# A mixture of 32 experts in 16 pairs: four places for a pair's rows, weights in 8 KB packets, another order at the end

## The chip, the cores and the metric

The kernel runs on one core of one Trainium2 chip. The metric is the device time of one execution in microseconds (us); lower is better. Engines are named as in the profile: PE multiplies matrices, PEld is its loading of weights, DVE and ACT work on vectors, POOL works on vectors and issues indirect DMAs, SP issues the other DMAs.

## The reference

One block for 512 tokens of width 1024, in float32: a state-space mixer and a latent attention side by side, a cross attention into 256 memory rows, a hierarchical mixture of experts, and a final norm. The change touches the last two:

```
x = x + _hier_moe(_rms(x, norm_moe_g), ...)
    # a token chooses 1 of 4 groups of experts, then 2 of the 8 experts in it; for each:
    # out += gate_weight * (silu(t @ w_gate[e]) * (t @ w_up[e])) @ w_down[e]
return _rms(x, norm_final_g)
```

An expert has w_gate and w_up of 1024 x 256 and w_down of 256 x 1024, 3 MB together, so 32 experts are 96 MB of weights. The final norm divides a row by the root of the mean of its squares and multiplies it by a gain.

## The kernel before

**Pairs.** The experts are worked in 16 pairs. Each expert has 64 places for tokens (`CAP`), so a pair has 128, one per partition. Which token has which place is found by the router; an index table `IX` says for each pair which rows of `hd` (the tokens in memory) to gather, `IY` where its results go. A token's first result goes to `xd` (which starts as x itself), the second to `yd`.

**Stages of a pair n.** `get` (L1768) transposes the gathered rows on PE (tile pX) and DVE copies them out with the gain (XT). `first` (L1780) multiplies by gate and up of both experts into pG (128 places by 512: 256 gate columns, 256 up columns); ACT takes SiLU of the gate half (sl, L1806), DVE multiplies by the up half (a, L1812). `second` transposes that (pA, L1830), ACT copies it out (aT, L1832), and PE multiplies by down (pD, L1846). DVE adds the rows that were already scaled (YY, L1855), except for pairs 14 and 15, whose sums are made on PE at the end. The main loop runs `first(n)`, then `second(n - 1)`, so that products of two pairs alternate on PE.

**Rows on POOL.** There are two places for gathered tokens, XG[0] and XG[1], and one tile YY with two halves for results (`result`, L1816). In `first(n)` POOL scales the tokens of pair n into their half of YY (L1808), then gathers the tokens of pair n + 2 into the place just read (L1699). `second(n - 1)` ends with two scatters of the half of YY to xd and yd (L1861). POOL does these in program order: scale, gather, scatter, scatter.

**Weights on SP.** `load_to` (L1303) issues the loads of weights on SP in a fixed turn, ahead of their use, into buffers that come free as PE is done with them. A tile `gu` holds half of the depth of both matrices: index c = 0 has k = 0 to 3 of each group of eight rows of gate and of up, c = 1 has k = 4 to 7. It takes two DMAs of 512 KB (L1310 gate, L1311 up) whose runs are 4 KB per partition. The down weights of an expert are one DMA of 1 MB (L1323) in runs of 8 KB, the last two of them in halves. One product step takes 64 places of one expert against 512 columns, gate and up at once (L1789), which the profile shows as two PE instructions.

**The end.** When the scatter of pair 13 has landed, `take_back` (L1872) reads yd and xd back, eight DMAs of 512 KB, and `both(t)` adds the two for each of four groups of 128 tokens, t = 0 to 3, on DVE (L1944). `last_sum` puts the results of pairs 14 and 15 onto the tokens with PE (pC; L1920, and for t = 2 and 3 also the tokens themselves by an identity, L1914). Then the order `TO` runs: a (L1929) adds pC to the tokens for t = 0, 1 in two halves; s takes squares and their sums on ACT (L329) half by half; o scales on DVE (L1940) and issues the output. Last, DVE copies the four pC tiles of t = 2, 3 into the tokens (L1961), for an expert that ran out of places; the branch for it is not taken in the profiled execution.

Of the kernel before, what the change touches and what calls it, by code (L numbers as in the profile page):

```python
# [15 lines left out]
AF = mybir.ActivationFunctionType  # L16
# [3 lines left out]
S = 512  # L20
# [42 lines left out]
OBJ = 3  # L63
OQ = '00-01-10-P2-11-20-C0-C1-C2-P3-C3-21-30-31'.split('-')
TQ = 1
TO = 'a00 s00 a01 s01 a10 s10 a11 s11 o00 o01 s20 s21 o10 o11 s30 s31 o20 o21 o30 o31'.split()
FH = 1
T1 = 1
CM = 1
# [4 lines left out]
PL0 = {(3,0):0,(3,2):1}  # L74
CP = 3
CB = 1
G1 = 6
FE = 0
LS = 0
LC = 2  # L80
# [24 lines left out]
def build(tc, I, out, dbg=None, stop=None):  # L105
# [1185 lines left out]
    def slot(tag, shape, name, dt=F32):  # L1291
        if tag == "A":
            return ua(shape, dt, name)
        if tag in "EG":
            return (E[0] if tag == "E" else GP_).tile(shape, dt, name=name, tag=tag)
        if tag in "FY":
            return MP.tile(shape, dt, name=name, tag=tag, bufs=NF if tag == "F" else 1)
        return u("H" if tag == "X" else tag, shape, dt, name)
# [3 lines left out]
    def load_to(n):  # L1302
        while nld[0] < min(n, 96):  # L1303
            i = turn[nld[0]]
            nld[0] += 1
            e, c = order[i]
            tag = tags[i]
            if c < 2:
                t = slot(tag, [128, 2, 4, 256], f"gu{e}{c}")
                nc.sync.dma_start(t[:, 0], wgt[e, :, 4 * c:4 * c + 4])  # L1310
                nc.sync.dma_start(t[:, 1], wup[e, :, 4 * c:4 * c + 4])  # L1311
            else:
                t = slot(tag, [128, 2, D], f"dn{e}")
                if i == 94:
                    late.append((t, e))
                    nc.sync.dma_start(t[:, :, 0:512], wdn[e][:, :, 0:512])
                elif i == 95:
                    late.append((t, e))
                    nc.sync.dma_start(t[:, :, 0:512], wdn[e][:, :, 0:512])
                    for t_, e_ in late:  # L1320
                        nc.sync.dma_start(t_[:, :, 512:D], wdn[e_][:, :, 512:D])
                else:
                    nc.sync.dma_start(t, wdn[e])  # L1323
            ew[e, c] = t
# [368 lines left out]
    if at("router"):  # L1693
        return

    stage = {}

    def gather(n):
        gat.append(nc.gpsimd.indirect_dma_start(out=XG[n % 2], out_offset=None, in_=hd,  # L1699
                                                in_offset=bass.IndirectOffsetOnAxis(ap=IX[:, n:n + 1], axis=0),  # L1700
                                                bounds_check=S - 1, oob_is_err=False))

# [53 lines left out]

    silu, YY, lastd = [None], [], {}
    turns = {}  # L1760

    def turn_(k, i):
# [3 lines left out]
    xts_ = {0: dict(enumerate(xt0))}  # L1766

    def get(n, c):  # L1768
        xg = XG[n % 2].rearrange("t (p k) -> t k p", k=8)
        ps = bankt(f"pX{n}{c}")  # L1770
        for k in range(4):
            i = nc.tensor.transpose(ps[:, k * 128:k * 128 + 128], xg[:, 4 * c + k], ident)  # L1772
            behind(i, last[0])
            behind(i, lastd.get(n - 2))
        if n == 1:
            last[0] = i
        xt = half_T(n, c)
        xts_.setdefault(n, {})[c] = xt
        evac_T(xt, ps, c)

    def first(n, mid=None):
        xt = xts_.setdefault(n, {})
        pg = bank2(f"pG{n}", "a") if n else bank("pG0")

        def mul(k0, k1):
            for k in range(k0, k1):
                c, kk = divmod(k, 4)
                for s in range(2):
                    i = nc.tensor.matmul(pg[64 * s:64 * s + 64], xt[c][:, kk, 64 * s:64 * s + 64],  # L1789
                                         ew[2 * n + s, c][:, :, kk], start=k == 0, stop=k == 7)  # L1790
                    behind(i, last[0])
            last[0] = i

        if n == 0:
            mul(0, G1)
            get(1, 0)
            mul(G1, 8)
        else:
            if n > 1:
                get(n, 0)  # L1800
            get(n, 1)
            if mid is not None:
                next(mid)
            mul(0, 8)
        sl = MP.tile([128, 256], F32, name=f"sl{n}", tag="sl", bufs=1)
        silu[0] = nc.scalar.activation(sl, pg[:, 0:256], AF.Silu, scale=RS[:, n:n + 1])  # L1806
        if 0 < n < NS:
            nc.gpsimd.tensor_scalar(result(n), XG[n % 2], F1[:, n:n + 1], 1.0, OP.mult, OP.mult)  # L1808
        if n and n + 2 < 16:
            gather(n + 2)  # L1810
        a = MP.tile([128, 2, 128], F32, name=f"a{n}", tag="a", bufs=1)
        stt.append(v.scalar_tensor_tensor(a.rearrange("s t p -> s p t"), pg[:, 256:512].rearrange("s (p t) -> s p t", t=2),  # L1812
                               RS[:, n:n + 1], sl.rearrange("s (p t) -> s p t", t=2), OP.mult, OP.mult))
        stage[n] = a

    def result(n):  # L1816
        if not YY:
            YY.append(slot("Y", [128, 2, D], "YY"))
        return YY[0][:, n % 2]

    def in_turn(n, i):
        if n > 13:
# [3 lines left out]
    def second(n):  # L1826
# [7 lines left out]
        if sums:  # L1834
            Y = slot(next(free), [128, 2, D], f"Y{n}", F32R)
            oht = MP.tile([128, S], F32R, name=f"oht{n}", tag="oht")
            v.tensor_scalar(oht, tokh, TK[:, n:n + 1], None, OP.is_equal)
            stage["y", n] = Y, oht
        else:
            Y = result(n)  # L1840
        yield at_i
        for c in range(2):
            pd = bank(f"pD{n}{c}")
# [81 lines left out]
    def fin_(k, t, c):  # L1925
        x = pc[t, c] if t in on_pe else X[t][:, half[c]]
        r = fst[:, 3, t:t + 1]
        if k == "a":
            turn_("v", v.tensor_tensor(x, x, pc[t, c], OP.add))  # L1929
        elif k == "s":  # L1930
            turn_("a", square_sum(fst[:, c, t:t + 1], x, spare[:, c]))
            if c == 0:
                turn_("a", nc.scalar.activation(fst[:, 2, t:t + 1], fst[:, 0, t:t + 1], AF.Copy, scale=1.0 / D, bias=EPS))
            else:
                turn_("a", nc.scalar.activation(r, fst[:, 1, t:t + 1], AF.Sqrt, scale=1.0 / D, bias=fst[:, 2, t:t + 1]))
        else:
            if c == 0:
                turn_("v", v.reciprocal(r, r))
            xg = (xg0, xg1)[c]
            turn_("v", v.scalar_tensor_tensor(xg[:, t], x, r, gf[:, half[c]], OP.mult, OP.mult))  # L1940
            nc.sync.dma_start(out[0, t * 128:t * 128 + 128, half[c]], xg[:, t])
# [5 lines left out]
    on_pe = (2, 3)  # L1947
    for i in down15:
        turn_("v", i)
    for t in range(NT):  # L1950
        both(t)
    for n, ts in ((14, (0, 1, 2, 3)), (15, (0, 1)), (None, (2,)), (15, (2,)), (None, (3,)), (15, (3,))):
        for t in ts:
            for c in range(2):
                last_sum(t, c, n)
    for q in TO:
        fin_(q[0], int(q[1]), int(q[2]))

    for t in on_pe:
        for c in range(2):  # L1960
            turn_("v", v.tensor_copy(X[t][:, half[c]], pc[t, c]))  # L1961
    overflow(*ov)
    es.close()

# [18 lines left out]
```

## Time and profile before

| what | value |
|---|---|
| time, median of 3 runs | 717.35 us (716.89 to 717.83) |
| the profiled execution: time | 717.67 us |
| its span | 715.9 us |
| its granted PE clock, mean | 0.984 |
| PE / DVE / ACT / POOL busy, share of the span | 93% / 57% / 35% / 16% |
| bytes by the hardware queue / the software queue | 157.58 MB / 7.58 MB |

The span is the time from the first to the last instruction of the profile; 1.8 us of the profiled execution lie outside it. The last of pair 15's products ends at about 686 us of the span. In the table by stretches the granted clock is a share of full speed. A wait in brackets is the idle time of the engine before the row, with the instruction whose end released it.

### The profile page before, as it was taken

Reading aid. Unit: us, or ns where it says so; the run is one execution under the profiler, and the core shown is the slowest. Engines: PE = TensorE matmul, PEld = TensorE weight load, DVE = VectorE, ACT = ScalarE, POOL = GpSimd, SP = SyncE. Lnnn points to the kernel's source line nnn. Section 1 sums busy time; section 2 is a strip of 40 time slices with the busy share of each in tenths; the row PEclk is TensorE's granted clock in tenths of the full one; section 3 lists DMA queues with packets and bytes.
Section 4 is the critical chain, followed back from the end, with each engine's and each line's share of the span. In section 5 each row is a group of like instructions: output and inputs, shape, how many; then the busy total and the mean of one; then the engine's idle time right before and its main releaser. Section 6 shows DMA issues by size and latency. Waiting matters only on the chain.

```text
span 715.9 us, 10163 instructions
## 1 busy us (share of the span) xinstructions
PE 666.9 (93%) x3644; PEld 469.7 (66%) x3644; DVE 406.1 (57%) x952; ACT 251.8 (35%) x518; POOL 113.7 (16%) x165
## 2 busy tenths in 40 slices
PE   5989999788999999999999999989999999999793
PEld 4788878676778888888887788734344454454342
DVE  4899988747577887565366642653443512221137
ACT  5734364325666767244344522221000000000023
POOL 6300022002400000102000001212242233233100
PEclk9999999989999999999999999999999999999988
DMA  7763233335452434323328797799999999999993
GB/s 217 199 197 99 66 79 95 79 124 125 112 191 67 147 120 118 95 83 89 91 87 314 274 334 276 240 395 410 405 412 406 411 412 404 410 411 409 381 356 128
DMA packets 102012, 165.83 MB, mean 232 GB/s; under 512 B 32762, under 2 KB 64606, under 8 KB 98120
## 3 DMA queue, kind: packets, MB, share of 16 engines
q1 hardware_dynamic: 95512, 157.58, 62.0%
q0 software_dynamic: 6432, 7.58, 3.1%
q8 instruction: 30, 0.49, 0.3%
q14 instruction: 22, 0.18, 0.1%
q10 hardware_dynamic: 16, 0.00, 0.0%
HBM read 154.59 MB, written 25.69 MB: 252 GB/s over the span
## 4 chain that ended last, share of the span: by engine, by line
PE 59%; DMA 28%; DVE 5%; ACT 4%; issue 1%; SPq 1%; POOL 1%; ACTq 0%; DVEq 0%
DMA gu<-moe_w_up 18%; DMA dn<-moe_w_down 6%; PE pG L1789 3%; PE po L1039 2%; PE pxq L268 2%; PE pxq L267 2%; PE pxq L266 2%; PE pxo L266 2%; DMA raw<-w_in 2%; PE pxo L267 2%; PE pD L1846 1%; PE pxo L268 1%; PE pcq L266 1%; PE pPT L1028 1%; PE pcq L267 1%
## 5 line engine op out<-in xcount | busy, mean ns | idle before, releaser
L1789 PE MATMUL pG<-gu,XT 128*64 128x512 f32 x512 | 120.3, 607 | 6.6 <-DMA gu<-moe_w_up 3.0
L214 DVE TENSOR_TENSOR lo<-raw,hi 128x1024 fp32r<-128x1024 f32 (+3 forms) x64 | 75.5, 1183 | 62.0 <-ACT hi L204 61.5
L204 ACT ACTIVATE hi<-raw 128x1024 fp32r<-128x1024 f32 (+3 forms) x64 | 63.9, 1002 | 107.9 <-issue 26.0
L1789 PEld LDWEIGHTS pG<-gu,XT 128*64 128x64 f32 x512 | 54.5, 139 | 58.7 <-issue 52.0
L1812 DVE SCALAR_TENSOR_TENSOR a<-pG,RS,sl 128x256 f32<-128x256 f32 x16 | 10.7, 671 | 113.2 <-ACT sl L1806 106.8
L1846 PE MATMUL pD<-dn,aT 128*64 128x512 f32 x256 | 71.1, 600 | 0.5 <-ACT aT L1832 0.5
L1806 ACT ACTIVATE sl<-pG,RS 128x256 f32<-128x256 f32 x16 | 7.6, 473 | 123.5 <-PE pG L1789 123.5
L1846 PEld LDWEIGHTS pD<-dn,aT 128*64 128x64 f32 x256 | 22.4, 137 | 35.7 <-issue 34.4
L1855 DVE SCALAR_TENSOR_TENSOR YY<-pD,GT,YY 128x512 f32<-128x512 f32 x26 | 19.5, 750 | 25.2 <-PE pD L1846 25.1
L1808 POOL TENSOR_SCALAR YY<-XG,F 128x1024 f32<-128x1024 f32 x13 | 14.5, 1116 | 114.8 <-issue 50.7
L1832 ACT ACTIVATE aT<-pA 128x256 f32<-128x256 f32 x16 | 6.1, 384 | 68.0 <-PE pA L1830 36.4
L1772 PEld LDWEIGHTS pX<-ident,XG 128*128 128x128 f32 x120 | 14.6, 194 | 16.9 <-issue 12.9
L267 PE MATMUL pxq<-gT,hi 128*128 128x512 f32 x64 | 25.6, 400 | 0.0
L266 PE MATMUL pxq<-gT,hi 128*128 128x512 f32 x64 | 25.5, 399 | 0.0
L268 PE MATMUL pxq<-gT,lo 128*128 128x512 f32 x64 | 25.4, 396 | 0.0
L1417 DVE TENSOR_TENSOR XT<-pX,gmo 128x512 f32<-128x512 f32 x30 | 19.3, 683 | 7.4 <-PE pX L1772 7.4
L1772 PE MATMUL pX<-ident,XG 128*128 128x128 f32 x120 | 17.6, 288 | 3.8 <-DMA XG<-hd,IX 3.8
L1388 POOL TENSOR_TENSOR st_moe<-st_moe 128x1 f32<-128x1 f32 x4 | 0.8, 190 | 118.6 <-issue 104.4
L266 PE MATMUL pcq<-hT,hi 128*128 128x512 f32 x48 | 19.2, 401 | 0.0
L268 PE MATMUL pcq<-hT,lo 128*128 128x512 f32 x48 | 19.1, 398 | 0.0
L267 PE MATMUL pxv<-lo,mT 128*128 128x512 f32 x32 | 13.9, 435 | 5.5 <-DVE lo L214 5.5
L267 PE MATMUL pcq<-hT,hi 128*128 128x512 f32 x48 | 18.9, 395 | 0.0
(614 smaller groups left out, 1670.6 us busy)
## 6 DMA issues: line engine op xcount, KB each, us to landing
gu<-moe_w_gate SPq DMA_DIRECT2D x64, 512.0 KB
gu<-moe_w_up SPq DMA_DIRECT2D x64, 512.0 KB
dn<-moe_w_down SPq DMA_DIRECT2D x30, 1024.0 KB
raw<-w_in SPq DMA_DIRECT2D x9, 512.0 KB
raw<-xattn_w_v SPq DMA_DIRECT2D x8, 512.0 KB
raw<-xattn_w_k SPq DMA_DIRECT2D x8, 512.0 KB
raw<-w_out SPq DMA_DIRECT2D x8, 512.0 KB
raw<-xattn_w_q SPq DMA_DIRECT2D x8, 512.0 KB
```

Source lines behind the costliest of these rows:

```text
L204: anchor["act"] = nc.scalar.activation(hi, r, AF.Copy)
L214: anchor["dve"] = nc.vector.tensor_tensor(lo, r, hi.bitcast(F32), OP.subtract)
L266: i = nc.tensor.matmul(o, lh, rh, start=start, stop=False)
L267: nc.tensor.matmul(o, lh, rl, start=False, stop=False)
L268: anchor["pe"] = nc.tensor.matmul(o, ll, rh, start=False, stop=stop)
L1039: nc.tensor.matmul(po[64 * s:64 * s + 64, b * 128:b * 128 + 128], V[:, k, 64 * h:64 * h + 64], PTs[s][:, k * 128:k * 128 + 128], start=k = ...
L1417: return v.tensor_tensor(xt, ps.rearrange("p (k t) -> p k t", k=4), gmo[:, 4 * c:4 * c + 4, None].to_broadcast([128, 4, 128]), OP.mult)
L1772: i = nc.tensor.transpose(ps[:, k * 128:k * 128 + 128], xg[:, 4 * c + k], ident)
L1789: i = nc.tensor.matmul(pg[64 * s:64 * s + 64], xt[c][:, kk, 64 * s:64 * s + 64], ew[2 * n + s, c][:, :, kk], start=k == 0, stop=k == 7)
L1808: nc.gpsimd.tensor_scalar(result(n), XG[n % 2], F1[:, n:n + 1], 1.0, OP.mult, OP.mult)
L1846: i = nc.tensor.matmul(pd[64 * s:64 * s + 64], at_[:, f, 64 * s:64 * s + 64], ew[2 * n + s, 2][:, f, c * 512:c * 512 + 512], start=f == 0, ...
L1855: yield v.scalar_tensor_tensor(o, pd, GT[:, n:n + 1], o, OP.mult, OP.add)
```

## The change

It has three parts.

**Four places.** `rows_(n)` names the place of pair n: XG[1], XG[0], and the two halves of YY, in turn. POOL scales the tokens where they lie, DVE adds the results in place, and the scatters read from there. The gather for pair n + 2 writes the place that pair n - 2 had.

```diff
+    def rows_(n):
+        return (XG[1], XG[0], *YY)[(n - 1) % 4]
...
-            nc.gpsimd.tensor_scalar(result(n), XG[n % 2], F1[:, n:n + 1], 1.0, OP.mult, OP.mult)
-        if n and n + 2 < 16:
+            if n == 1:
+                yy = slot("Y", [128, 2, D], "YY")
+                YY.extend(yy[:, i] for i in range(2))
+                nc.gpsimd.memset(YY[0], 0.0)
+                gather(3)
+            nc.gpsimd.tensor_scalar(rows_(n), rows_(n), F1[:, n:n + 1], 1.0, OP.mult, OP.mult)
+        if 1 < n < 14:
             gather(n + 2)
```

POOL's order in the middle of the stage, before. XG0 and XG1 are the two places for tokens, YY is the tile of results, hd the tokens in memory, xd and yd the two targets:

```order
L1808 TENSOR_SCALAR YY_4962<-XG1_4699,F1_4793 128x1024
L1699 DMA XG1_4699<-hd_4130,IX_4789 128x1024
L1861 DMA xd_4131<-YY_4962,IY_4792 512x1024
L1861 DMA yd_716<-YY_4962,IY_4792 512x1024
L1808 TENSOR_SCALAR YY_4962<-XG0_4698,F1_4793 128x1024
L1699 DMA XG0_4698<-hd_4130,IX_4789 128x1024
L1861 DMA xd_4131<-YY_4962,IY_4792 512x1024
L1861 DMA yd_716<-YY_4962,IY_4792 512x1024
```

And the same place now:

```order
L1816 TENSOR_SCALAR XG1_4684<-XG1_4684,F1_4777 128x1024
L1701 DMA YY_4974<-hd_4130,IX_4773 128x1024
L1864 DMA xd_4131<-YY_4974,IY_4776 512x1024
L1864 DMA yd_716<-YY_4974,IY_4776 512x1024
L1816 TENSOR_SCALAR XG0_4683<-XG0_4683,F1_4777 128x1024
L1701 DMA YY_4974<-hd_4130,IX_4773 128x1024
L1864 DMA xd_4131<-XG1_4684,IY_4776 512x1024
L1864 DMA yd_716<-XG1_4684,IY_4776 512x1024
```

The order of kinds is the same; the operands moved. Before, the scaling writes a half of YY, from which the scatters of two pairs earlier must have read; now it writes its own input, and it is the gather behind it whose target those scatters have read.

**Weights.** A tile `gu` holds one whole matrix, gate for c = 0 and up for c = 1, in one DMA of 1 MB with 8 KB per partition. The products run over gate first, then over up, in 256 columns each; for pair 0 the first tokens of pair 1 are transposed between the two.

```diff
-                t = slot(tag, [128, 2, 4, 256], f"gu{e}{c}")
-                nc.sync.dma_start(t[:, 0], wgt[e, :, 4 * c:4 * c + 4])
-                nc.sync.dma_start(t[:, 1], wup[e, :, 4 * c:4 * c + 4])
+                t = slot(tag, [128, 8, 256], f"gu{e}{c}")
+                nc.sync.dma_start(t, (wgt, wup)[c][e])
...
-        def mul(k0, k1):
-            for k in range(k0, k1):
-                c, kk = divmod(k, 4)
-                for s in range(2):
-                    i = nc.tensor.matmul(pg[64 * s:64 * s + 64], xt[c][:, kk, 64 * s:64 * s + 64],
-                                         ew[2 * n + s, c][:, :, kk], start=k == 0, stop=k == 7)
-                    behind(i, last[0])
+        def mul(*cs):
+            for c in cs:
+                for k in range(8):
+                    for s in range(2):
+                        i = nc.tensor.matmul(pg[64 * s:64 * s + 64, 256 * c:256 * c + 256],
+                                             xt[k // 4][:, k % 4, 64 * s:64 * s + 64], ew[2 * n + s, c][:, k],
+                                             start=k == 0, stop=k == 7)
+                        behind(i, last[0])
             last[0] = i

         if n == 0:
-            mul(0, G1)
+            mul(0)
             get(1, 0)
-            mul(G1, 8)
+            mul(1)
```

`G1` was 6. SP's queue has 64 DMAs fewer.

**The end.** The order `TO` and the additions on DVE change, squares of t = 0, 1 are taken over 1024 columns at once (S, with its own square root), and the four copies of pC move from DVE to ACT.

```diff
-TO = 'a00 s00 a01 s01 a10 s10 a11 s11 o00 o01 s20 s21 o10 o11 s30 s31 o20 o21 o30 o31'.split()
+TO = 'a00 a01 S00 a10 a11 S10 o00 o01 s20 s21 o10 o11 s30 s31 o20 o21 o30 o31'.split()
...
+        elif k == "S":
+            turn_("a", square_sum(fst[:, 1, t:t + 1], X[t], spare.rearrange("p c d -> p (c d)")))
+            turn_("a", nc.scalar.activation(r, fst[:, 1, t:t + 1], AF.Sqrt, scale=1.0 / D, bias=fst[:, 2, t:t + 1]))
...
-    for t in range(NT):
+    nc.gpsimd.memset(fst[:, 2, 0:2], EPS)
+    for t in range(3):
         both(t)
...
+    for q in TO[:2]:
+        fin_(q[0], int(q[1]), int(q[2]))
+    both(3)
...
-            turn_("v", v.tensor_copy(X[t][:, half[c]], pc[t, c]))
+            turn_("a", nc.scalar.activation(X[t][:, half[c]], pc[t, c], AF.Copy))
```

DVE's order at the end, before; the four xb are the tokens of t = 0 to 3:

```order
L1944 TENSOR_TENSOR xb_6162<-xb_6162 128x1024
L1944 TENSOR_TENSOR xb_6165<-xb_6165 128x1024
L1944 TENSOR_TENSOR xb_6168<-xb_6168 128x1024
L1944 TENSOR_TENSOR xb_6171<-xb_6171 128x1024
L1929 TENSOR_TENSOR xb_6162<-xb_6162,pC_6262 128x512
L1929 TENSOR_TENSOR xb_6162<-xb_6162,pC_6265 128x512
L1929 TENSOR_TENSOR xb_6165<-xb_6165,pC_6268 128x512
L1929 TENSOR_TENSOR xb_6165<-xb_6165,pC_6271 128x512
```

And now:

```order
L1950 TENSOR_TENSOR xb_6339<-xb_6339 128x1024
L1950 TENSOR_TENSOR xb_6342<-xb_6342 128x1024
L1950 TENSOR_TENSOR xb_6345<-xb_6345 128x1024
L1932 TENSOR_TENSOR xb_6339<-xb_6339,pC_6455 128x512
L1932 TENSOR_TENSOR xb_6339<-xb_6339,pC_6458 128x512
L1950 TENSOR_TENSOR xb_6348<-xb_6348 128x1024
L1932 TENSOR_TENSOR xb_6342<-xb_6342,pC_6461 128x512
L1932 TENSOR_TENSOR xb_6342<-xb_6342,pC_6464 128x512
```

The addition for t = 3 has moved behind the first two additions of pC. The matrix products of `last_sum` for t = 2, 3 were put in the same order behind those for t = 0, 1.

More of the change, by code (lines that the diff above doesn't have):

```diff
@@ L76 @@
 CB = 1
-G1 = 6
 FE = 0
@@ L1694, in build @@
         return
-    stage = {}
+    stage, YY = {}, []
+    def rows_(n):
+        return (XG[1], XG[0], *YY)[(n - 1) % 4]
     def gather(n):
-        gat.append(nc.gpsimd.indirect_dma_start(out=XG[n % 2], out_offset=None, in_=hd,
+        gat.append(nc.gpsimd.indirect_dma_start(out=rows_(n), out_offset=None, in_=hd,
                                                 in_offset=bass.IndirectOffsetOnAxis(ap=IX[:, n:n + 1], axis=0),
@@ L1755, in overflow @@
                     nc.sync.dma_start(out[0, t * 128:t * 128 + 128, half[c]], o[:, t])
-    silu, YY, lastd = [None], [], {}
+    silu, lastd = [None], {}
     turns = {}
@@ L1768, in get @@
     def get(n, c):
-        xg = XG[n % 2].rearrange("t (p k) -> t k p", k=8)
+        xg = rows_(n).rearrange("t (p k) -> t k p", k=8)
         ps = bankt(f"pX{n}{c}")
@@ L1803, in first @@
                 next(mid)
-            mul(0, 8)
+            mul(0, 1)
         sl = MP.tile([128, 256], F32, name=f"sl{n}", tag="sl", bufs=1)
@@ L1814, in first @@
         stage[n] = a
[L1816 to L1819, printed above, removed]
     def in_turn(n, i):
@@ L1839, in second @@
         else:
-            Y = result(n)
+            Y = rows_(n)
         yield at_i
@@ L1949, in build @@
         turn_("v", i)
-    for t in range(NT):
+    nc.gpsimd.memset(fst[:, 2, 0:2], EPS)
+    for t in range(3):
         both(t)
-    for n, ts in ((14, (0, 1, 2, 3)), (15, (0, 1)), (None, (2,)), (15, (2,)), (None, (3,)), (15, (3,))):
+    for n, ts in ((14, (0, 1, 2, 3)), (15, (0, 1))):
         for t in ts:
@@ L1955, in build @@
                 last_sum(t, c, n)
-    for q in TO:
+    for q in TO[:2]:
+        fin_(q[0], int(q[1]), int(q[2]))
+    both(3)
+    for t in on_pe:
+        for n in (None, 15):
+            for c in range(2):
+                last_sum(t, c, n)
+    for q in TO[2:]:
         fin_(q[0], int(q[1]), int(q[2]))
```

## The prediction

> **What bounds the kernel now.** I read the table by stretches first, for the stage in which the experts run. Its columns are the stretch, its length, then the busy time of PE, PEld, DVE, ACT and POOL with instruction counts, and at the end the granted clock, the busy share of the DMA engines and GB/s.
>
> ```profile
> 480.00:500.00 20.00, 18.79 (x98) 7.88 (x100) 6.14 (x20) 3.14 (x7) 4.85 (x4) 1.00 1.02 406
> 640.00:660.00 20.00, 19.20 (x85) 9.82 (x84) 5.37 (x9) 1.24 (x3) 8.36 (x8) 1.00 1.03 412
> 660.00:680.00 20.00, 16.24 (x66) 6.67 (x65) 3.51 (x6) 0.86 (x2) 1.95 (x2) 0.97 1.00 383
> ```
>
> Two resources are full at once: the DMA engines (share 1.00 to 1.03, 406 to 412 GB/s) and PE (18.8 and 19.2 of 20 us). A gain in one pays only until the other binds. The chain that ended last says which of them did at the end:
>
> ```profile
> 667.00 12.48 DMA gu<-moe_w_up
> 679.62 6.10 PE pG L1789 x13
> 699.30 1.89 PE pC L1914 x4
> 701.67 0.69 DVE xb L1929
> 711.05 2.48 DVE xb L1961 x4
> ```
>
> The last up weights land at 679.6, the products of pair 15 follow, the combination pC, the final norm, four copies. The PE timeline around it tells how near the two resources are (start, length, instructions, and in brackets the idle time before):
>
> ```profile
> 670.61 1.16 PE L1772 MATMUL pX<-ident,XG 128*128 128x128 f32 x8
> 672.12 4.50 PE L1789 MATMUL pG<-gu,XT 128*64 128x512 f32 x18 [0.35 <-DVE XT L1417]
> 679.62 6.10 PE L1789 MATMUL pG<-gu,XT 128*64 128x512 f32 x13 [3.00 <-DMA gu<-moe_w_up]
> 685.56 0.59 PE L1789 MATMUL pG<-gu,XT 128*64 128x512 f32 x1
> ```
>
> PE came to pair 15 at 670.61 and waited only 3.00 us for weights. So earlier weights buy at most about 3 us there, and more only because the 13 instructions after the wait took 6.10 us, where 32 take 7.09 in pair 3 (row below): with the wait the slow spell may go too. The same 3 us are lost again if PE itself comes later.
>
> The third party is POOL, which scales the tokens of a pair, gathers those of the next but one and scatters results. In its timeline the first number is the start:
>
> ```profile
> 508.30 1.13 POOL L1808 TENSOR_SCALAR YY<-XG,F 128x1024 f32<-128x1024 f32 x1 [8.76 <-DMA yd<-YY,IY]
> 509.88 1.08 POOL L1699 DMA_INDIRECT XG<-hd,IX  x1 [0.46 <-POOL YY L1808]
> 512.59 0.99 POOL L1861 DMA_INDIRECT yd<-YY,IY  x1 [0.30 <-issue]
> 520.79 1.11 POOL L1808 TENSOR_SCALAR YY<-XG,F 128x1024 f32<-128x1024 f32 x1 [7.21 <-DMA yd<-YY,IY]
> ...
> 601.21 1.08 POOL L1699 DMA_INDIRECT XG<-hd,IX  x1 [0.28 <-POOL YY L1808]
> 614.37 1.11 POOL L1808 TENSOR_SCALAR YY<-XG,F 128x1024 f32<-128x1024 f32 x1 [9.48 <-issue]
> ...
> 654.84 1.11 POOL L1808 TENSOR_SCALAR YY<-XG,F 128x1024 f32<-128x1024 f32 x1 [7.78 <-issue]
> 656.23 1.09 POOL L1699 DMA_INDIRECT XG<-hd,IX  x1 [0.28 <-PE pX L1772]
> ```
>
> It is a ring: scale, gather, scatter, wait until the scatter has landed, scale again. From 508.30 to 654.84 there are 11 turns, 13.3 us each, of which scale and issue take 1.4 to 1.6 us (508.30 to 509.88). The view of DMA issues gives the landings:
>
> ```profile
> XG<-hd,IX POOLq DMA_INDIRECT x15, 7.8
> yd<-YY,IY POOLq DMA_INDIRECT x14, 9.6
> ```
>
> Gather 15, issued at 656.23, thus lands near 664.0, six us before PE wants it. That is the reserve of the ring.
>
> **Part 1, packets of 8 KB.** The DMA view by short windows counts packets per queue (q1 carries weights, q0 gathers and scatters; last column: share of 16 engines). The first window, 472 to 475, has 8 KB weight packets alone, the second, 510 to 513, 4 KB ones, the third, 514 to 520, 4 KB ones beside one gather and its two scatters:
>
> ```profile
> DMA packets 170, 1.27 MB, mean 422 GB/s; under 512 B 16, under 2 KB 16, under 8 KB 17
> q1 hardware_dynamic: 167, 1.23, 99.9%
> ```
> ```profile
> DMA packets 345, 1.25 MB, mean 416 GB/s; under 512 B 41, under 2 KB 41, under 8 KB 344
> ```
> ```profile
> q1 hardware_dynamic: 499, 1.97, 81.0%
> q0 software_dynamic: 431, 0.49, 23.1%
> ```
>
> 422 against 416 GB/s is 0.036 us per MB. Another window of 4 KB packets at 408 would make it 0.085:
>
> ```profile
> DMA packets 334, 1.22 MB, mean 408 GB/s; under 512 B 36, under 2 KB 36, under 8 KB 333
> ```
>
> I take 0.06. With some 50 MB of gate and up weights after 460, this is 3.0 us (1.8 to 4.3): the last weights land at 676.6 instead of 679.6.
>
> But in the third window 431 software packets went past 499 hardware packets: the queues nearly alternate, one for one. A hardware packet there took 81.0% of 6 us times 16 engines over 499, 0.156 us; in the first window 99.9% of 3 us times 16 over 167, 0.287 us. A trio of gather and two scatters is 431/16 = 27 packets per engine. With an 8 KB neighbour at each turn it takes 27 x 0.131 = 3.5 us longer. Its whole turn from gather to landed scatter was 10.9 us (509.88 to 520.79) beside 4 KB packets alone, and 13.2 (601.21 to 614.37), where the weights in flight were partly 8 KB ones of down. So 13.2 is the floor for the new turn, 10.9 + 3.5 = 14.4 its working value, 10.9 + 31 x 0.131 = 15.0 (a hardware packet for every one of 499/16) the top. I take 14.2, as stretches with an empty weight queue spare some turns.
>
> **Part 2, four places in turn.** The scaling is done in place and waits for nothing late: it drops out of the ring. The gather now waits for the scatters two pairs back, which sit behind the gather before it in POOL's queue. The ring is 14.2 then, against 13.3: the removed 1.4 to 1.6 us do not quite pay for the longer packets. It starts at 508.2 (the landing for which the scaling at 508.30 waits), and gather 15 is the 11th after gather 4: 508.2 + 11 x 14.2 = 664.4. Its landing takes 7.8 plus a third of 3.5, 9.0 us: 673.4. PE had begun pair 15 at 670.61. The reserve is used up. Behind the waiting gather POOL holds only the scatters of the pair before, whose results nobody reads until SP's reading back at the end. At pair 1 a memset takes the place of the scaling ahead of gather 3, at no cost. On SP 64 issues fewer cost and bring nothing that I can see.
>
> **Part 3, products in halves of 256 columns.** 64 PE instructions a pair in place of 32. The nearest rows for 256 columns:
>
> ```profile
> 387.46 0.28 PE L266 MATMUL pxs<-xK,xQ 128*128 128x256 f32 x1
> ...
> 388.75 0.28 PE L268 MATMUL pxs<-xK,xQ 128*128 128x256 f32 x1
> ...
> 509.46 7.09 PE L1789 MATMUL pG<-gu,XT 128*64 128x512 f32 x32 [0.17 <-DVE XT L1417]
> ```
>
> 11 steps in 1.29 us are 0.117 each, with weight loads 128 wide. Half of a 512-column step of today (7.09 less the last 0.59, over 31: 0.210) is 0.105. So a pair costs between 0 and 64 x 0.012 = 0.8 us more; loads here are 64 wide, half the size, so I take 0.2, 2.8 us over 14 pairs. The Trainium skill ("TensorE: Matmul & The Clock Gate", Back-to-back issue gap) gives N / 2.4 + 2.5 ns, 109 ns for 256 columns: 64 x (109 - 105) would be 0.25 us a pair. The row of 0.117 is dearer than that rule.
>
> For pair 0 the split matters once more:
>
> ```profile
> 476.86 1.93 PE L1789 MATMUL pG<-gu,XT 128*64 128x512 f32 x6
> 480.62 0.68 PE L1772 MATMUL pX<-ident,XG 128*128 128x128 f32 x4 [1.83 <-DMA XG<-hd,IX]
> 481.23 1.94 PE L1789 MATMUL pG<-gu,XT 128*64 128x512 f32 x8
> PE pX L1772 <- DMA XG<-hd,IX: 3.8, 3, 1.8
> ```
>
> Only 8 of 32 instructions come behind the wait for gather 1; now half will. That adds 8 x 0.21 = 1.7 us of work after it. The other two gather waits (3.8 less 1.8) are 2.0 us, which go if the gathers come sooner. PE's own arrival at pair 15 is then 670.6 + 1.7 + 2.8 - 2.0 = 673.1, beside 673.4 by the gathers. Two arrivals so close push one another; I take 674.5. SiLU needs only gate now and starts half a product earlier; four pD instructions already cover that wait, so I cost it at nothing.
>
> From 674.5: 1.5 us to the first product (670.61 to 672.12) and 7.1 for all of them, end 683.1. The up half is wanted from 679.6, three us after it lands at 676.6, so the wait and its slow spell go. Today's end is 686.15 (685.56 + 0.59): **-3.0 us**.
>
> **Part 4, the end.**
>
> ```profile
> SPq L1872 <- DMA yd<-YY,IY: 6.1, 1, 6.1
> 671.75 0.98 POOL L1861 DMA_INDIRECT xd<-YY,IY  x1 [11.83 <-DVE YY L1855]
> 700.53 1.23 DVE L1944 TENSOR_TENSOR xb<-xb 128x1024 f32<-128x1024 f32 x1 [1.39 <-DMA xb<-xd]
> 702.39 0.63 ACT L329 ACTIVATE fin<-xb 128x512 f32<-128x512 f32 x1 [8.12 <-DVE xb L1929]
> L1857 ACT ACTIVATE YY<-pD,GT x2: 687/687/687, 493.9 to 495.6; 128x512 f32<-128x512 f32 x2
> ```
>
> SP holds the reading back of xd and yd until the scatter of pair 13 has landed; that one follows PE and shifts by some 2 us with it. Today the first addition of the end (701.67) also stands behind the last of four sums (700.53 + 1.23). With both(3) put behind a00 and a01, three of four suffice: two of the eight 512 KB reads fewer, 2 x 1.28 us at 410 GB/s. So this side gives +2.0 - 2.6 = -0.6, and the products -3.0, but the weights have left the DMA engines 3 us earlier when the reads go. I take **-2.5** for the first addition. The one-pass square starts after two additions (0.69 more) and does two halves and one accumulator read fewer: two tiles in about 4.1 against 702.39 - 701.67 plus two tiles at 1.8, 4.3: **-0.2**. The copies leave DVE, where they ended at 713.53, for ACT, idle from about 709.5, four at 0.69, end 712.3; the last output transfer sets the end then: **-0.4**.
>
> **Sum.** -2.5 - 0.2 - 0.4 = -3.1 against the profiled execution (717.67, span 715.9): 714.6, and by the median shown (717.35) 714.2. I predict 714.2.
>
> **Rivals.** *The alternating queues pace the kernel (slower).* With the ring at 15.0 gather 15 is issued at 508.2 + 165 = 673.2, lands at 682.2, products end at 682.2 + 8.6 = 690.8, 4.6 later than today; less 0.6 at the end is +4.0: 721.4. It decides from a ring of (686.15 + 0.6 - 8.6 - 9.0 - 508.2)/11 = 14.6 us. For it: the counts 431 and 499, and 13.2 us already with part of the packets large. Against it: PE that waits frees buffers later, the weight queue runs dry and the trio speeds up. Of the like speaks the Trainium skill ("DMA: Bandwidth & Descriptors", Queues, rings and completion order): an engine takes turns between its queues, a whole packet at a time. By it alone the ring would stand at its upper value; the trace's counts agree with the turns.
>
> *The shorter steps do not run at half price (slower).* At 0.117 a step, PE is 14 x 0.8 = 11.2 later instead of 2.8, pair 15 starts at 681.5, products end 690.1: +3.9 - 0.6, 720.6.
>
> *The gathers keep their reserve (faster still).* At 13.2 a turn and no dearer steps, products end with the weights, 676.6 + 3.6 = 680.2 to 681; the end then starts 5 to 6 us sooner: 711.3, and 709.5 if PE's slow spell behind pair 15 goes as well.
>
> *Cancelling.* Ring near 14.6: within 0.2% (1.4 us, about what a measurement tells from none) of 717.35.
>
> **Chances.** Forecast with the third rival 0.56 (0.40 and 0.16), cancelling 0.09, alternating queues 0.25, dear steps 0.10. The likeliest case's own range is 711.5 to 715.8; with the others at both ends 709.5 to 721.4 leaves out about 2 in 10.
>
> **What would show it.** Right: scale instructions without waits for yd, gathers 14 to 14.4 us apart, gather 15 issued near 664, no wait of PE for up at pair 15, the last weights near 676.6. Wrong: PE waits for XG in most pairs, gathers 15 us or more apart; or 64 products that take over 7.6 us; or weights no earlier than 679 with PE waiting for them, which would void the gain of the packets.

## The result and the profile after

The changed kernel takes 726.03 us (median of 4 runs, 723.34 to 727.13), the kernel before 717.59 beside it. The ratio estimated from these runs is 1.0105, interval 1.0082 to 1.0127 (the two medians alone divide to 1.0118): slower by about 1%. The profiled execution took 727.13 us with a span of 725.3, against 717.67 and 715.9.

The table by stretches of the changed kernel (columns as before) shows two things at once. From 520 to 660 the DMA engines move 415 to 418 GB/s, where it was 406 to 412. But at 480 to 500 the DMA engines stood idle for a fifth of the time, PE ran at a granted clock of 0.83 there, and later PE is not full in several stretches:

```profile
480.00:500.00 20.00, 18.14 (x128) 10.36 (x130) 4.75 (x17) 2.07 (x5) 3.14 (x3) 0.83 0.78 297
560.00:580.00 20.00, 16.67 (x126) 9.50 (x124) 8.12 (x24) 1.05 (x3) 7.34 (x8) 0.91 1.02 418
640.00:660.00 20.00, 19.54 (x110) 9.84 (x107) 4.89 (x7) 1.33 (x3) 6.23 (x6) 1.00 1.02 415
680.00:700.00 20.00, 19.65 (x142) 11.14 (x138) 4.19 (x7) 1.33 (x3) 5.02 (x5) 1.00 0.45 156
```

The last row, beside a DMA share of 0.84 there before, says that the DMA engines had little left to load by then: loading no longer limits the end. What does, the chain that ended last of the changed kernel says. Where weights stood, scatters stand:

```profile
549.13 11.86 DMA yd<-YY,IY
...
564.47 11.02 DMA yd<-YY,IY
...
639.87 11.56 DMA yd<-XG,IY
...
654.91 11.34 DMA yd<-XG,IY
...
667.03 8.60 DMA XG<-hd,IX
...
691.59 7.13 PE pG L1791 x64
```

Each piece marked yd is a scatter from its issue until it has landed, and a gather starts 0.78 us behind it. POOL's timeline of the changed kernel shows the ring itself. The idle time of 11 of its 12 gathers from gather 4 on ends with the landing of yd; for gather 4, the first row, this view names a copy on DVE, but the chain that ended last has a scatter to yd there too (503.61 to 514.62):

```profile
515.60 1.08 POOL L1701 DMA_INDIRECT YY<-hd,IX  x1 [9.80 <-DVE XT L1415]
...
546.43 1.09 POOL L1701 DMA_INDIRECT XG<-hd,IX  x1 [10.06 <-DMA yd<-XG,IY]
547.83 1.00 POOL L1864 DMA_INDIRECT xd<-YY,IY  x1 [0.31 <-issue]
549.13 0.99 POOL L1864 DMA_INDIRECT yd<-YY,IY  x1 [0.30 <-issue]
550.13 1.16 POOL L1816 TENSOR_SCALAR XG<-XG,F 128x1024 f32<-128x1024 f32 x1
561.77 1.08 POOL L1701 DMA_INDIRECT YY<-hd,IX  x1 [10.48 <-DMA yd<-YY,IY]
...
682.38 1.09 POOL L1701 DMA_INDIRECT YY<-hd,IX  x1 [10.52 <-DMA yd<-YY,IY]
```

From gather 4 at 515.60 to gather 15 at 682.38 there are 11 turns of 15.16 us on average (14.3 to 16.1); before they were 13.3. The scaling does start without a wait now. PE waits for tokens in all 12.8 + 3.5 us against 3.8 before, and for no weights. The number behind the name is the sum, then how many waits, then the longest:

```profile
PE pX L1774 <- DMA XG<-hd,IX: 12.8, 6, 4.8
PE pX L1774 <- DMA YY<-hd,IX: 3.5, 2, 3.2
```

Pair 15's products end at 698.72 (691.59 + 7.13), 12.6 us later than before (686.15); from there to the end of the span the kernel needs 26.6 us instead of 29.75. So 12.6 are lost and 3.2 come back: 9.4, the difference of the spans. At pair 15 itself PE did not wait for tokens: its last such wait was 0.80 us for gather 14 (the piece at 667.03 in the chain), and pair 15 followed at PE's own pace, 14.3 us a pair (675.77 to 690.08). A ring of 15.16 is slower than that pace, so PE has to wait for it again and again, eight times in all.

### The profile page after: what moved, and what is told of

It reads as the page before. It is cut to its first block, busy times and chain, and to the rows that moved or that the text cites. A ratio compares the mean times of both kernels' runs of the same rounds, so it can differ in the third digit from the quotient of the medians.

```text
span 725.3 us, 11069 instructions
## 1 busy us (share of the span) xinstructions
PE 669.8 (92%) x4156; PEld 495.5 (68%) x4156; DVE 406.3 (56%) x948; ACT 253.6 (35%) x516; POOL 115.2 (16%) x167
## 4 chain that ended last, share of the span: by engine, by line
PE 56%; DMA 22%; issue 7%; DVE 5%; ACT 4%; POOL 3%; SPq 1%; POOLq 0%; DVEq 0%; ACTq 0%
DMA yd<-XG,IY 10%; DMA yd<-YY,IY 6%; DMA XG<-hd,IX 2%; PE po L1038 2%; PE pG L1791 2%; PE pxq L265 2%; PE pxq L266 2%; PE pxq L267 2%; PE pD L1849 2%; PE pxo L265 2%; DMA raw<-w_in 2%; PE pxo L266 2%; PE pxo L267 1%; PE pcq L265 1%; PE pPT L1027 1%
## 5 line engine op out<-in xcount | busy, mean ns | idle before, releaser
L1791 PE MATMUL pG<-gu,XT 128*64 128x256 f32 x1024 | 122.1, 397 | 3.2 <-issue 2.1
L1791 PEld LDWEIGHTS pG<-gu,XT 128*64 128x64 f32 x1024 | 80.8, 143 | 40.0 <-issue 10.0
L1849 PE MATMUL pD<-dn,aT 128*64 128x512 f32 x256 | 69.6, 598 | 0.5 <-ACT aT L1835 0.5
L1849 PEld LDWEIGHTS pD<-dn,aT 128*64 128x64 f32 x256 | 20.8, 136 | 33.8 <-issue 31.8
L1415 DVE TENSOR_TENSOR XT<-pX,gmo 128x512 f32<-128x512 f32 x30 | 19.5, 686 | 19.8 <-PE pX L1774 12.7
L1774 PE MATMUL pX<-ident,XG 128*128 128x128 f32 x64 | 10.6, 312 | 12.8 <-DMA XG<-hd,IX 12.8
L1774 PEld LDWEIGHTS pX<-ident,XG 128*128 128x128 f32 x64 | 8.6, 198 | 19.2 <-issue 14.4
L1701 POOL DMA_INDIRECT XG<-hd,IX x8 | 8.8, 1105 | 63.9 <-DMA yd<-XG,IY 62.2
L265 PE MATMUL pxk<-mT,hi 128*128 128x256 f32 x64 | 18.9, 295 | 0.0
```

Source lines behind the costliest of these rows:

```text
L265: i = nc.tensor.matmul(o, lh, rh, start=start, stop=False)
L1415: return v.tensor_tensor(xt, ps.rearrange("p (k t) -> p k t", k=4), gmo[:, 4 * c:4 * c + 4, None].to_broadcast([128, 4, 128]), OP.mult)
L1701: gat.append(nc.gpsimd.indirect_dma_start(out=rows_(n), out_offset=None, in_=hd, in_offset=bass.IndirectOffsetOnAxis(ap=IX[:, n:n + 1], ax ...
L1791: i = nc.tensor.matmul(pg[64 * s:64 * s + 64, 256 * c:256 * c + 256], xt[k // 4][:, k % 4, 64 * s:64 * s + 64], ew[2 * n + s, c][:, k], st ...
L1849: i = nc.tensor.matmul(pd[64 * s:64 * s + 64], at_[:, f, 64 * s:64 * s + 64], ew[2 * n + s, 2][:, f, c * 512:c * 512 + 512], start=f == 0, ...
```

## The experiments

Each run has its own runs of the kernel before on the same chip beside it; their medians lie between 717.67 and 718.42, and ratios are against these. Labels are those of the expectations.

| label | edit | us | ratio to before, interval |
|---|---|---|---|
| e_order0 | changed kernel, pair 0 split as before | 722.15 | 1.0064 (1.0045 to 1.0082) |
| e_4k | changed kernel, 4 KB packets | 718.27 | 1.0011 (0.9991 to 1.0031) |
| e_swap | gather written behind the scatters | 725.87 | 1.0111 (1.0068 to 1.0154) |
| e_end | before, with the end alone | 715.53 | 0.9967 (0.9949 to 0.9986) |
| e_swap2 | gather held behind the scatters | 731.56 | 1.0173 (1.0134 to 1.0212) |
| e_order0_swap2 | gather held, and pair 0 split as before | 729.46 | 1.0148 (1.0114 to 1.0182) |
| e_places | before, with four places alone | 717.70 | 0.9992 (0.9974 to 1.0011) |
| e_order0_4k | changed, pair 0 as before, 4 KB | 714.34 | 0.9947 (0.9928 to 0.9967) |
| e_old_places | changed, without the four places | 734.14 | 1.0230 (1.0200 to 1.0260) |
| e_order0_six | changed, pair 0 as before, six places | 719.64 | 1.0017 (0.9998 to 1.0035) |
| e_six_held | the same, gathers held to their step | 715.74 | 0.9972 (0.9951 to 0.9993) |
| e_six_late | the same, one clearing left out, one moved | 713.34 | 0.9933 (0.9907 to 0.9959) |

**e_order0: what the start costs.**

```diff
             mul(0)
+            mul(1, ks=range(0, 4))
             get(1, 0)
-            mul(1)
+            mul(1, ks=range(4, 8))
```

> The changed kernel with one edit: for pair 0 half of the up products (8 of 16 steps) come ahead of the transposes of pair 1 again, so 24 of 32 steps of pair 0 lie ahead of the wait for gather 1, as before the change. Theory S (the start): PE's 4.82 us of idle time there fell to about 3, the slow clock behind it goes, SiLU of pair 0 starts near 484 instead of 488.3, the scatter of pair 0 lands some 5 us earlier, and since the ring of gathers runs from that landing to the end, the time falls by 4 to 5 us: 721 to 722. Rival R (the ring is set by something else than its start, by the weights or PE): the shift is swallowed on the way, 724 to 726.

722.15, 3.9 us under the changed kernel: the start does cost about what theory S says, and R falls, but theory S's account of it holds only in part. First the changed kernel's PE timeline around gather 1 (32 steps come behind it), then that of this run (16):

```profile
481.38 1.09 PE L1774 MATMUL pX<-ident,XG 128*128 128x128 f32 x4 [4.82 <-DMA XG<-hd,IX]
482.40 5.83 PE L1791 MATMUL pG<-gu,XT 128*64 128x256 f32 x32
488.81 7.13 PE L1791 MATMUL pG<-gu,XT 128*64 128x256 f32 x64
```
```profile
480.37 1.09 PE L1774 MATMUL pX<-ident,XG 128*128 128x128 f32 x4 [3.41 <-DMA XG<-hd,IX]
481.38 3.68 PE L1791 MATMUL pG<-gu,XT 128*64 128x256 f32 x16
```

32 instructions in 5.83 us are 0.18 each, 64 in 7.13 are 0.11. In the table by stretches of the changed kernel the clock behind the wait is 0.60. The loads run dry there too: SP issues none between 475.65 and 488.26, waiting for PE's products to free buffers:

```profile
481.40:488.20 6.80, 6.80 (x37) 3.89 (x37) 0.69 (x1) 0.00 (x0) 0.00 (x0) 0.60 0.52 213
```

The slow clock came here too, contrary to the expectation: 16 in 3.68 are 0.23 each, behind a wait of 3.41. The gain came from the shorter wait and from half the steps being left to do at that price: pair 0's SiLU starts at 485.14, 3.2 us sooner and not the 4.3 expected. The ring started 2.6 us sooner (gather 4 at 513.05 instead of 515.60) and turned a little faster (14.94). So of the 5.0 us by which gather 15 is issued sooner (677.41 instead of 682.38), about half comes from the start and half from the turns, which the theory did not have; why they were shorter no run shows.

**e_4k: what the packets cost.**

```diff
-                nc.sync.dma_start(t, (wgt, wup)[c][e])
+                for h in range(2):
+                    nc.sync.dma_start(t[:, 4 * h:4 * h + 4], (wgt, wup)[c][e][:, 4 * h:4 * h + 4])
```

> The changed kernel with one edit: each gate or up matrix comes in two DMAs of 512 KB with runs of 4 KB per partition instead of one of 1 MB with 8 KB; products, places and end stay. Theory P (hardware and software packets take turns one for one, so the size of the weight packets sets how long a trio of gather and scatters takes): the ring falls from 15.2 to 12.5 to 13.2 us a turn, PE no longer waits for gathers behind pair 8, the time falls to 718 to 721 (the late start of 5 us stays, the weights come at 408 to 412 GB/s again). Rival Q (the ring is long because the gather waits for the scatters at all, whatever the packets): ring 15, time 725 to 727.

718.27, 7.8 us under the changed kernel, with the same places, products and waits in the program. Theory P holds, Q falls. PE waits for tokens only once, 3.5 us at pair 1. The ring turns in 12.85 us on average (gathers 4 to 15 from 513.36 to 654.73); POOL's timeline of this run has one of its shortest turns, 11.5 us, where the changed kernel has 15.9:

```profile
513.36 1.08 POOL L1702 DMA_INDIRECT YY<-hd,IX  x1 [8.61 <-DVE XG L1859]
...
524.86 1.08 POOL L1702 DMA_INDIRECT XG<-hd,IX  x1 [6.64 <-DMA yd<-XG,IY]
```

The packets of the two queues say why. First the changed kernel, 553 to 559, then this run, 517 to 523, each six microseconds in which the packets of a trio, a gather with its two scatters, are moving:

```profile
q1 hardware_dynamic: 314, 2.29, 91.7%
q0 software_dynamic: 307, 0.16, 9.3%
```
```profile
q1 hardware_dynamic: 525, 1.99, 81.9%
q0 software_dynamic: 424, 0.48, 22.8%
```

Beside 8 KB packets 307 software packets went past 314 hardware ones, beside 4 KB packets 424 past 525. Nearly one for one either way, and the larger the hardware packet (91.7% of 6 us times 16 engines over 314 is 0.28 us, 81.9% over 525 is 0.15), the fewer turns in the same time. A whole trio has 432 software packets. Counted in windows of a quarter of a microsecond, those of this trio of the changed kernel move from 550.75 to 560.0, in 9.25 us; those of the trio of e_4k from 517.65 to 523.65, in 6.0.

**e_end: the end alone**, the last part of the change's diff on the kernel before.

> The kernel before with the end part alone (order at the end, one-pass squares, copies on ACT). Nothing ahead of 690 moves. Theory E (the first addition waited for the fourth sum, 701.67, and needs only three): the first addition near 699.3, time down by 1.5 to 2.5 us, 715 to 716. Rival (the matrix products of the end, or the last transfers, set it anyway): within 0.7 us of 717.6.

715.53, 2.1 us under the 717.67 beside it, by the interval 1.0 to 3.7. The time is that of theory E, the mechanism only in part, as DVE's timeline of this run shows:

```profile
700.39 1.28 DVE L1929 TENSOR_TENSOR xb<-xb,pC 128x512 f32<-128x512 f32 x2
701.86 1.23 DVE L1947 TENSOR_TENSOR xb<-xb 128x1024 f32<-128x1024 f32 x1 [0.19 <-DMA xb<-xd]
703.00 1.28 DVE L1929 TENSOR_TENSOR xb<-xb,pC 128x512 f32<-128x512 f32 x2
```

The first additions go ahead of the fourth sum, at 700.39 instead of 701.67, and not at 699.3. But the additions for t = 1 still stand behind that sum and its transfer, and the squares of t = 1 wait for them. In the profiled execution, one of the longer of this run's ten (717.20), the span is only 0.6 under that of the kernel before (715.3); which of the three edits of the end brings the 2.1, no run tells.

**e_swap: an edit that did nothing.** The call of the gather was moved behind the scatters in the program.

> The changed kernel with one edit: on POOL the gather for pair n + 2 stands behind the two scatters of pair n - 1 instead of ahead of them. It still waits for the scatters of pair n - 2, but these were issued a pair of PE time earlier and no scatter stands behind that wait. Theory P: the ring opens, POOL waits for PE and not for landings, gathers arrive 9 us after their issue and 13 us before use or just in time, PE waits for gathers under 4 us in all, time 714 to 719. Rival (software queue short of throughput: a trio of 15 us cannot be run every 14): time stays above 723, and scatters land later and later.

725.87, the changed kernel's own time. The engine's order explains it: the scheduler, the part of the tools that puts the instructions of an engine in order before the run, sorted the gather ahead of the scatters again, row for row as in the changed kernel. So this run tells nothing of either theory, only that the time repeats. The next one holds the order.

**e_swap2 and e_order0_swap2: the gather behind the scatters.**

```diff
             for i in down:
...
+            if 1 < n < 14:
+                gather(n + 2)
+                behind(gat[-1], scat[-1])
```

> The changed kernel with the gather for pair n + 2 held behind the two scatters of pair n - 1 on POOL by an order dependency (in the run before, the scheduler had left the order as it was). The gather still waits for the scatters of pair n - 2, which now have a whole pair's time for landing. Theory P: the ring opens, POOL's gathers go at PE's pace, PE waits for gathers under 6 us in all instead of 16, the products of pair 15 end near 685 to 688 instead of 698.7, time 713 to 717. Rival T (the software queue lacks throughput beside 8 KB packets, not only latency): scatters land later and later, gathers still come late, time above 721.

> Both repairs on the changed kernel: the gather behind the scatters on POOL, and 24 of 32 steps of pair 0 ahead of the wait for gather 1. Theory: the two losses lie in one row, so the gains add: 4 us under the run with the gather moved alone, 709 to 713, faster than the kernel before. Rival: with the ring open PE or the reading back at the end sets the time and the start is absorbed, within 1.5 us of the run with the gather moved alone.

731.56 and 729.46: theory P failed, and its rival's time came true without its account: scatters did not land later and later (the last of e_order0_swap2 beside full weight traffic, issued at 663.74, took 10.5 us, the one at 525.97 as much). The pair-0 edit alone still gains 2.1 us here, not 4 and over the rival's 1.5. POOL's timeline of e_swap2:

```profile
577.97 1.03 POOL L1701 DMA_INDIRECT YY<-hd,IX  x1 [0.30 <-issue]
579.04 1.12 POOL L1816 TENSOR_SCALAR YY<-YY,F 128x1024 f32<-128x1024 f32 x1
587.38 1.03 POOL L1862 DMA_INDIRECT xd<-XG,IY  x1 [7.21 <-DVE XG L1856]
588.71 0.98 POOL L1862 DMA_INDIRECT yd<-XG,IY  x1 [0.30 <-issue]
590.00 1.03 POOL L1701 DMA_INDIRECT XG<-hd,IX  x1 [0.30 <-issue]
```

No gather waits for a landing any more; POOL waits for results of PE and DVE. But the gather now goes last of its trio, and with 8 KB packets beside it the last lands 10.9 to 12.7 us after its issue, the first 8.0 to 8.6 (the gathers of e_order0_swap2 against those of the changed kernel whose landing the trace has). Its issue moved behind the products with down of the pair before, so it comes too late for PE by another way: PE waits 12.1 + 8.0 us for tokens in e_swap2, more than in the changed kernel. A ring through PE replaced the ring through the scatters.

**e_places: four places alone**, the first part of the diff on the kernel before.

> The kernel before with the four places alone (loads of 4 KB packets, products of 512 columns and the end as before). Theory: beside 4 KB packets the ring was never far from PE's pace; the scaling leaves it, a turn falls from 13.3 to 11.5 to 12.5 us, PE's waits for gathers at pairs 8 and 9 (2.0 us) go, but the weights still land at 679 or so: 715.5 to 717.7. Rival (places cost by themselves: the gather's new wait): slower than 719.

717.70 against 718.42, no difference: the time is as expected. The turn is not: beside mixed packets, 4 KB of gate and up and 8 KB of down, it is 13.0 us (gathers 4 to 15 from 508.98 to 652.28), not 11.5 to 12.5. In the chain that ended last loads of weights stand, not the ring.

**e_order0_4k: both losses taken away.**

> The changed kernel with 4 KB packets (two DMAs of 512 KB per matrix) and pair 0's order as before. Theory: packets and start are the two losses, so what is left of the change is its gains, the end (2.1 us in the run of the end alone) and little else: 714 to 716.5. Rival: products in halves or whole matrices as units of loading cost by themselves: 717.5 or more.

714.34, ratio 0.9947: faster than the kernel before. The two repairs alone gave 3.9 and 7.8 us, together 11.7 (726.03 to 714.34). What remains of the change is worth 0.5%, and the end alone has 0.3%; the two intervals overlap, so it is not shown that anything but the end is left.

**e_old_places: what the four places gave.** The changed kernel with the old scaling from XG into YY.

> The changed kernel with the two places for tokens and one tile of results of the kernel before; 8 KB packets, products in halves, pair 0's split and the end as changed. Theory P: scale (1.12 us) and its issue are back in the ring, 1.4 us a turn over 11 turns on the chain that ends last: ring 16.5, time 738 to 743. Rival (the scaling was hidden beside the landing anyway): 725 to 728.

734.14, 8 us over the changed kernel, less than theory P expected and more than the rival. Without the four places the changed kernel is 2.3% slower than the kernel before, and not 1%. The ring rose only to 15.75 (gathers 4 to 14 from 515.98 to 673.44), 0.6 instead of 1.4 over the changed kernel's 15.14 for the same gathers. A piece of this run's chain and two rows of its POOL timeline show most of the reason:

```profile
644.46 11.73 DMA yd<-YY,IY
```
```profile
656.38 1.11 POOL L1807 TENSOR_SCALAR YY<-XG,F 128x1024 f32<-128x1024 f32 x1 [10.94 <-DMA yd<-YY,IY]
657.77 1.08 POOL L1697 DMA_INDIRECT XG<-hd,IX  x1 [0.28 <-POOL YY L1807]
```

The scatter has landed at 656.19 and the scaling starts 0.19 us later; scaling and its issue take 1.39. In the changed kernel the gather waits for the landing itself, and starts 0.78 us behind it (549.13 + 11.86 = 560.99, gather at 561.77). So taking the scaling out of the ring saves 1.39 less 0.59, 0.8 us a turn, and not 1.4.

**e_order0_six, e_six_held and e_six_late: more places.** Six places in turn; the two more are paid with one of the weight buffers (NF 1 for 2).

```diff
-NF = 2
+NF = 1
...
-        return (XG[1], XG[0], *YY)[(n - 1) % 4]
+        return (XG[1], XG[0], *YY)[(n - 1) % 6]
```

> The changed kernel, 8 KB packets kept, with six places in turn instead of four (the space comes from one of the weight buffers, NF 1 instead of 2) and pair 0's order as before. A gather for pair n + 2 waits for the scatters of pair n - 4, two pairs back from those of pair n - 2; POOL's order is not changed. Theory P in its latency form (a trio takes 15 us because it is chained to the next one, and 10 us of packets fit into a pair): the chain opens, gathers go at PE's pace, PE waits for gathers under 4 us in all, the products of pair 15 end at 680 to 683, time 710 to 713. Theory T (throughput: beside 8 KB packets the software queue cannot move a trio each 14 us): gathers late again from the middle of the stage, 718 or more.

719.64: in the range of theory T, but not by its account, since no gather came late. PE no longer waits for gathers, and pair 15's SiLU starts at 682.44 instead of 698.77. But the scheduler had used the new places to gather two pairs further ahead, so each gather still waited for the trio just issued, as POOL's timeline of this run shows:

```profile
514.65 1.08 POOL L1701 DMA_INDIRECT Y<-hd,IX  x1 [12.46 <-DMA yd<-Y,IY]
...
529.31 1.08 POOL L1701 DMA_INDIRECT XG<-hd,IX  x1 [9.82 <-DMA yd<-XG,IY]
```

The ring had moved its cost to the scatters, and with them to the reading back at the end (PE waited 5.2 us for its sums). So the gather was held to its step:

```diff
-            nc.gpsimd.tensor_scalar(rows_(n), rows_(n), F1[:, n:n + 1], 1.0, OP.mult, OP.mult)
+            ts = nc.gpsimd.tensor_scalar(rows_(n), rows_(n), F1[:, n:n + 1], 1.0, OP.mult, OP.mult)
...
             gather(n + 2)
+            behind(gat[-1], ts)
```

> The run with six places again, but each gather held behind the scaling of its own step by an order dependency: in the run before, the scheduler used the two places for gathering two pairs further ahead, so a gather waited for the scatters of the trio just issued as ever, and the chain of trios stayed at 15 us a turn (the last scatters landed at 691, the reading back waited for them, PE 5.2 us for it). Now a gather waits for scatters that were issued two pairs before. Theory L (the trio's latency, chained, is the cost): trios go at PE's pace, POOL waits for PE, the scatters of pair 13 land near 684, the products of pair 15 end near 682, time 711 to 714.5. Theory T (throughput of the software queue beside 8 KB packets): trios of successive pairs overlap and stretch each other, gathers late, time 718 or more.

715.74, ratio 0.9972: T falls. Theory L's account holds (pair 15's SiLU starts at 682.49), its time by 1.2 us not. The same 8 KB packets beside the same software packets, one trio for each 12 to 15 us, and none waits for a landing. POOL's timeline of this run has the gather right behind the scaling and waits for PE's work alone:

```profile
586.51 1.15 POOL L1819 TENSOR_SCALAR YY<-YY,F 128x1024 f32<-128x1024 f32 x1
587.84 1.08 POOL L1701 DMA_INDIRECT Y<-hd,IX  x1 [0.17 <-issue]
598.75 1.01 POOL L1868 DMA_INDIRECT xd<-XG,IY  x1 [9.83 <-DVE XT L1415]
```

Its gather 1 was issued at 475.35, 3.3 us later than in the changed kernel, behind the clearing of two new places. In the last run one of the two clearings is left out, as pair 0's results fill that place, and the other stands behind gather 3:

```diff
-                for y in (YY[0], YY[2], YY[3]):
-                    nc.gpsimd.memset(y, 0.0)
+                nc.gpsimd.memset(YY[0], 0.0)
                 gather(3)
+                behind(nc.gpsimd.memset(YY[2], 0.0), gat[-1])
```

> The run with six places and held gathers, with one edit: of the two clearings of new places, which stood on POOL ahead of gather 1 and moved it from 472.1 to 475.4, one is left out (pair 0's results fill that place) and the other stands behind gather 3. All three parts of the change are in it, with 8 KB packets. Theory: gather 1 is issued near 472 again and the stage starts 2 to 3 us sooner; PE was ahead of the last weights in the run before (it waited 5.7 us for weights in all), so only part of it arrives: 713 to 715.5, under the kernel before. Rival: the DMA engines set the end altogether, 715 to 716.5, no change against the run before.

713.34, ratio 0.9933, gather 1 at 472.13 again: in the theory's range, 1.7 us under the low end of its rival's. It has all parts of the change with 8 KB packets, except that pair 0 is split as before, and two places more; it is faster than both kernels. Its chain ends in weights of down and the reading back, so loading sets the end again:

```profile
665.15 18.78 DMA dn<-moe_w_down
683.95 10.28 DMA xb<-xd
```

## Why the prediction was wrong, point by point

It forecast 714.2 with 0.56 on faster; the kernel is slower, and 726.03 lies beyond the range's end at 721.4. The rival of the alternating queues is what happened; it had 0.25. Its own 721.4 fell short, mostly by the start of pair 0 below.

**The step that failed: a turn of the ring at 14.2 us**, "as stretches with an empty weight queue spare some turns". There were no such stretches: the DMA share is 1.01 to 1.02 from 500 to 660, and the queues went 314 to 307. The turn was 15.16, above even the 15.0 that the prediction called the top. The counting was right: 3.5 us more for a trio's packets were worked out, and 9.25 against 6.0 us were counted. Two things below it were not. The discount from 14.4 to 14.2 had no ground, and one term was put at nothing: that POOL starts a gather 0.78 us after the landing it waits for, where the scaling had started 0.19 after it. So the four places take 0.8 us out of a turn and not the 1.4 to 1.6 of the prediction, and 14.4 + 0.6 = 15.0 would have been its own working value. It was decisive, since the rival's own condition was a turn of 14.6. By the Trainium skill's rule ("DMA: Bandwidth & Descriptors", Queues, rings and completion order), taking turns packet by packet, the trace agrees as to the turns.

**The term that was mis-sized: pair 0**, 1.7 us. SiLU of pair 0 started 5.07 us later (488.31 against 483.24). The prediction counted the steps behind gather 1 but not that PE, with those ahead of it gone, would wait 4.82 us instead of 1.83 and do the rest at a clock of 0.60. Part of that wait is gather 1 itself, which took 9.2 us to land instead of 8.0 and landed 0.8 us later. The Trainium skill ("TensorE: Matmul & The Clock Gate", What's actually happening) puts the slow clock behind about 3.4 us of idle PE; here it followed waits of 4.82 and 3.41 us, and in the kernel before one of 3.00, a little under the page's figure. Gather 4 was issued at 515.60, where the prediction lets the ring start at 508.2: 7.4 us, of which the start explains 5; the rest is the first scatter, which took 11.0 us to land instead of 9.6, and 1.0 us until POOL went on.

Together these two give the error of the issue of gather 15, 682.38 for the 664.4 forecast: 7.4 us by the start of the ring, 10.6 by 11 turns of 15.16 instead of 14.2. Of these 18.0 us, 15.6 reached the end of pair 15's products (698.72 for 683.1).

**Right in kind, near the low end in size:** the weights. From 500 to 660 they and all else moved at 416 GB/s against 409, which is 0.04 us per MB where 0.06 was taken from a range of 0.036 to 0.085, and PE waited for none. The gain had nowhere to go, since PE and not the weights came late to pair 15. That e_six_late is 0.67% faster than the kernel before, e_end 0.33%, leaves room for such a gain, but their intervals overlap, and its own size was not measured apart.

**Right in kind, smaller:** the steps of 256 columns. 64 of them take 7.13 us, 32 of 512 took 7.09, so 0.04 a pair, not 0.2, and 0.111 us a step. That rival, at 0.117, is out. The 109 ns that the prediction took from the Trainium skill ("TensorE: Matmul & The Clock Gate", Back-to-back issue gap) were nearer than the row of 0.117 with its wider loads.

**Larger than forecast, and not in its parts:** the end. The prediction has pair 15's products 3.0 us earlier and the whole 3.1, so from the products to the end of the span it gains 0.1; the changed kernel gained 3.2 there. All of it lies ahead of the first addition of pC (710.95, 12.2 us behind the products instead of 15.5). Some 2.0 of it are waits of DVE for the transfers read back (0.59 and 1.39 before, none now), which here are issued when the DMA engines have little else to move; another 1.2 is the fourth sum, which no longer stands ahead. From the first addition to the end of the span nothing was gained, 14.35 against 14.23: the 0.2 for squares and the 0.4 for copies did not show.

**The removed wait** of the scaling was worth something, but only against the longer packets: nothing beside the old loads (e_places), 8 us beside the new (e_old_places). The prediction's sentence that the 1.4 us do not quite pay for the packets was true, and by more than it said: 13.3 became 15.16, not 14.2.

## What to carry to other kernels

In this kernel a larger packet on one DMA queue was a longer turn for every small transfer on another (0.28 us a packet instead of 0.15, one trio's packets in 9.25 us instead of 6.0). Where such transfers form a ring (gather, work, scatter, and back to the same place), price the ring as packets times turn from the two queues' counts, take the full price as long as the engines are saturated, add the time from a landing to the start of what waits for it, and compare the sum with the pace of what it feeds. If it is too long, open the chain with more places rather than reorder within it, and look at the engine's order afterwards: twice here the scheduler turned an edit into another one.

When work is moved from ahead of a wait to behind it, count the idle time that it leaves and the clock behind it, not the moved steps alone.

## What the runs showed of the hardware that was not expected

A wait of PE of 3.0 to 4.8 us was followed by steps at about half speed for 4 to 6 us: 5.83 us for 32 instructions behind 4.82, 3.68 for 16 behind 3.41. One of 1.83 us (pair 0 of the kernel before) was not. The granted clock in these stretches, first of the kernel before behind its wait of 3.00, then of e_order0 behind 3.41, is the third number from the right:

```profile
679.60:686.00 6.40, 6.38 (x17) 2.07 (x19) 0.00 (x0) 0.00 (x0) 0.00 (x0) 0.54 0.89 331
```
```profile
480.00:485.00 5.00, 4.63 (x21) 2.44 (x21) 0.76 (x2) 0.00 (x0) 0.00 (x0) 0.50 0.81 332
```

A software DMA's time to land depended on its place among its neighbours: in the middle of the stage, beside 8 KB packets, the first of a trio took 7.6 to 9.1 us (changed kernel, e_order0 and e_order0_swap2), the last 10.9 to 12.7, whether that was the gather or the scatter to yd; with the weight queue empty (the last two scatters of e_order0, issued at 686.5 and 687.7) 3.2 and 3.0.
